# The w_o projection of an encoder block wholly as block products, and two weight sums moved into the FFN

## The chip, the cores and the metric

The kernel runs on one core of one Trainium2 chip. The metric is the device time of one execution in microseconds. A comparison of two kernels is made from several executions of each on the same chip.

## The reference

One trunk layer over 512 frames of 1024 features, in float32:

```python
xn = rmsnorm(h, norm_mix_g)
q, k, v, xr, gr, ga, gb = split(xn @ w_in)
ya = chunked_band_attention(q, k, v, rel_table) @ w_attn_out      # 16 heads of 64
yb = (rg_lru(causal_depthwise_conv(xr, ...)) * gelu(gr)) @ w_rnn_out
h = h + (sigmoid(ga) * ya + sigmoid(gb) * yb) @ w_o               # w_o: 1024 x 1024
g, up = split(rmsnorm(h, norm_ffn_g) @ w_ffn_in)                  # 2 x 2816 columns
h = h + (silu(g) * up) @ w_ffn_out
out = rmsnorm(h, final_norm_g)
```

The change concerns the line with w_o, the norm behind it, and where in time some sums of blocks of w_o and w_ffn_out are made.

## The kernel before

All of it is one program on one core. Products of float32 matrices are made of three passes: an operand is split into a rounded part (hi, by ScalarE, L82) and the rest (lo, by VectorE, L83), and `mm3` (L76 to L78) issues hi x hi, hi x lo, lo x hi on the tensor engine (PE). So every weight block goes through a load by SyncE's queue (SP) into a raw buffer, a split on ScalarE (ACT), a split on VectorE (DVE), and then PE. The raw buffers of the pool wp number three and are used in turn: a load is issued once the split (or the last sum) that read the block three loads earlier is done. Split blocks, called whl, have four buffers in wp, and during the w_o product four more in the pool wop.

Several products are made as block products: a pair of 256-row slices (a "unit") is cut in 2 x 2 blocks, and seven products of blocks or of sums of blocks stand for eight. The sums over the activations (s1 to s4) are made on the spot; the sums over the weights (t1 to t4) are made far ahead by `spill`: four blocks are loaded, four subtractions of 128x1024 run on DVE, and the four results are stored to DRAM, from where `wo_part` or `fo_part` loads them later. Before the change five such spills are made: for the units 0 and 1 of w_ffn_out in the recurrent stage, for w_o and unit 2 of w_ffn_out beside the rnn output product (yb), and for unit 3 beside the attention output product (ya).

The w_o product has 512 tokens (four tiles of 128) and 1024 columns (two halves). Its first 512 rows are a unit, by block products (`h_multiply`); its last 512 rows (two slices, i = 2 and 3) are plain (`plain_h`, `whl_wo`). A bank po_h per token tile and half gathers the sums and `h_read` or `finish_h` adds it to h. Where a token tile has both halves, ACT squares it (hj), DVE adds the two sums (hsq), ACT takes the root (sd), DVE the reciprocal (rs) and scales the tile's rows (xs_ffn, in `scaled`). `turned` then transposes xs_ffn two feature tiles at a time into a bank pt_ffn (two such banks take turns), and ACT and DVE evict it as hn (hi and lo) and x (the whole value). The first FFN products (po_f, weights fg0 and fu0) follow, and the block products of the FFN behind them (p_fg, q_fg, p_fu, q_fu), each with its sums s_fg, s_fu of weight blocks on DVE.

On PE the order is written by hand in the blocks under `manual_schedule`. The order on ACT, DVE and SP is a scheduler's, from the order of the code and its own estimates; each engine runs its rows strictly in that order.

## Time and profile before

| | us |
|---|---|
| median of 3 runs (863.87 to 864.8) | 864.19 |
| the profiled execution's own time | 864.16 |
| its span, first to last instruction | 862.4 |
| PE busy | 850.9 |
| DVE busy | 620.8 |
| ACT busy | 501.7 |

The span and all busy times come from one profiled execution. Lines L.. are those of the kernel; many share the helpers' lines L76 to L83, so groups are told apart by the names of their tiles. A matmul's length in the profile is longer than the distance to the next one, since matmuls overlap.

### The profile page before, as it was taken

The numbers are of one execution on the slowest core, as the hardware profiler recorded it, in microseconds if no ns is written. First come the engines' busy times: TensorE is split into PE (matmuls) and PEld (weight loads), VectorE is DVE, ScalarE is ACT, GpSimd is POOL, SyncE is SP. The second block draws the span as 40 slices with busy tenths as digits, with TensorE's granted clock in tenths as the row PEclk, the third lists the DMA queues.
The fourth block names the chain that finished last, engine by engine and source line by source line (L and its number), as shares of the span: only waits on it lengthen the run. The fifth ranks groups of instructions, "written<-read, shape, count | busy, mean of one in ns | idle before, by whom it ended". The sixth has DMA issues, their size and how long they took to land.

```text
span 862.4 us, 12989 instructions
## 1 busy us (share of the span) xinstructions
PE 850.9 (99%) x4908; PEld 745.6 (86%) x4908; DVE 620.8 (72%) x960; ACT 501.7 (58%) x862; POOL 98.2 (11%) x135
## 2 busy tenths in 40 slices
PE   8999999999999999999999999999999999999996
PEld 6977887888888888888888889999999999988885
DVE  5789866645666666556568968898878887389973
ACT  7577697741366656666634455656556556274543
POOL 2013203200113313223200000000000001000011
PEclk9999999999999999999999999999999999999999
DMA  8585323329842213233187621434333333295602
GB/s 270 183 309 171 98 74 107 113 88 358 271 139 74 73 41 120 74 90 96 49 300 254 202 74 47 126 97 124 104 115 100 99 98 101 82 315 170 195 18 97
DMA packets 93870, 118.91 MB, mean 138 GB/s; under 512 B 6256, under 2 KB 71392, under 8 KB 93808
## 3 DMA queue, kind: packets, MB, share of 16 engines
q1 hardware_dynamic: 90128, 110.42, 39.5%
q10 hardware_dynamic: 3680, 7.67, 2.9%
q8 instruction: 38, 0.62, 0.3%
q14 instruction: 24, 0.20, 0.1%
HBM read 105.45 MB, written 12.62 MB: 137 GB/s over the span
## 4 chain that ended last, share of the span: by engine, by line
PE 95%; ACT 1%; DVE 1%; issue 1%; DMA 1%; SPq 0%; DVEq 0%; ACTq 0%
PE po_out L76 4%; PE po_out L77 4%; PE po_out L78 4%; PE o L745 2%; PE p_fg L78 2%; PE p_fg L77 2%; PE p_fg L76 2%; PE p_fu L78 2%; PE p_fu L77 2%; PE p_fu L76 2%; PE pT L725 2%; PE po_ga L76 2%; PE po_v L76 2%; PE po_ga L78 2%; PE po_q L76 2%; PE po_ya L76 2%
## 5 line engine op out<-in xcount | busy, mean ns | idle before, releaser
L714 POOL TENSOR_SCALAR p<-p,rl 128x128 f32<-128x128 f32 (+1 forms) x64 | 39.6, 638 | 166.4 <-DVE rl L712 166.3
L711 ACT ACTIVATE p<-p,m 128x128 f32<-128x128 f32 (+1 forms) x64 | 35.8, 562 | 14.5 <-DVE m L710 14.5
L1057 POOL TENSOR_TENSOR act_lo<-act,act_hi 128x1024 fp32r<-128x1024 f32 x1 | 2.4, 2405 | 297.2 <-DVE s_fu L175 297.2
L83 DVE TENSOR_TENSOR pp<-pT,pp 128x384 fp32r<-128x384 f32 (+1 forms) x48 | 27.8, 596 | 9.8 <-ACT pp L82 9.7
L710 DVE CUSTOM_DVE_ANT_0 p<-s,bias 128x128 f32<-128x128 f32 (+1 forms) x64 | 29.2, 483 | 3.9 <-PE s L707 3.8
L83 DVE TENSOR_TENSOR whl_qk<-raw_qk,whl_qk 128x1024 fp32r<-128x1024 f32 x16 | 21.5, 1346 | 11.3 <-ACT whl_qk L82 11.3
L82 ACT ACTIVATE whl_fg_s<-s_fg 128x1024 fp32r<-128x1024 f32 x20 | 20.9, 1055 | 14.5 <-PE q_fg L78 5.3
L76 PE MATMUL po_gr<-xnT,whl_gr 128*128 128x512 f32 (+1 forms) x80 | 28.1, 352 | 0.1
L83 DVE TENSOR_TENSOR whl_fu_s<-s_fu,whl_fu_s 128x1024 fp32r<-128x1024 f32 x20 | 24.2, 1224 | 5.3 <-ACT whl_fu_s L82 5.3
L77 PE MATMUL po_xr<-xnT,whl_xr 128*128 128x512 f32 (+1 forms) x80 | 27.8, 353 | 0.0
L77 PE MATMUL po_gr<-xnT,whl_gr 128*128 128x512 f32 (+1 forms) x80 | 27.7, 348 | 0.0
L78 PE MATMUL po_gr<-xnT,whl_gr 128*128 128x512 f32 (+1 forms) x80 | 27.5, 348 | 0.0
L78 PE MATMUL po_xr<-xnT,whl_xr 128*128 128x512 f32 (+1 forms) x80 | 27.3, 346 | 0.0
L76 PE MATMUL po_xr<-xnT,whl_xr 128*128 128x512 f32 (+1 forms) x80 | 26.7, 352 | 0.6 <-ACT xnT L353 0.6
L83 DVE TENSOR_TENSOR whl_fg_s<-s_fg,whl_fg_s 128x1024 fp32r<-128x1024 f32 x20 | 24.2, 1223 | 3.6 <-ACT whl_fg_s L82 3.6
L82 ACT ACTIVATE whl_qk<-raw_qk 128x1024 fp32r<-128x1024 f32 x16 | 16.8, 1051 | 15.6 <-DMA spill<-in_w_ffn_out_dram 7.1
L76 PE MATMUL po_gb<-xnT,whl_gb 128*128 128x512 f32 x64 | 25.1, 393 | 0.5 <-DVE sp_p L452 0.3
L76 PE MATMUL po_ga<-xnT,whl_ga 128*128 128x512 f32 x64 | 25.3, 395 | 0.0
L77 PE MATMUL po_gb<-xnT,whl_gb 128*128 128x512 f32 x64 | 25.2, 394 | 0.0
L83 DVE TENSOR_TENSOR whl_t<-raw_t,whl_t 128x1024 fp32r<-128x1024 f32 x20 | 24.4, 1220 | 1.1 <-ACT whl_t L82 1.0
L78 PE MATMUL po_gb<-xnT,whl_gb 128*128 128x512 f32 x64 | 25.0, 391 | 0.0
L76 PE MATMUL po_q<-xnT,whl_qk 128*128 128x512 f32 x64 | 25.0, 391 | 0.0
(401 smaller groups left out, 3234.4 us busy)
## 6 DMA issues: line engine op xcount, KB each, us to landing
raw_fg<-in_w_ffn_in_dram SPq DMA_DIRECT2D x24, 512.0 KB, 3.5
raw_fu<-in_w_ffn_in_dram SPq DMA_DIRECT2D x22, 512.0 KB, 3.6
spill<-in_w_ffn_out_dram SPq DMA_DIRECT2D x16, 512.0 KB, 6.3
sums<-spill SPq DMA_DIRECT2D x16, 512.0 KB, 3.6
raw_qk<-in_w_in_dram SPq DMA_DIRECT2D x32, 256.0 KB, 3.3
raw_t<-sums SPq DMA_DIRECT2D x16, 512.0 KB, 4.5
raw_b<-in_w_ffn_out_dram SPq DMA_DIRECT2D x12, 512.0 KB, 4.4
raw_xr<-in_w_in_dram SPq DMA_DIRECT2D x8, 512.0 KB, 4.4
```

What stands on the lines that cost most here:

```text
L76: pe.matmul(o, sh, mh, start=start, stop=False, skip_group_check=parts)
L77: pe.matmul(o, sh, ml, start=False, stop=False, skip_group_check=parts)
L78: pe.matmul(o, sl, mh, start=False, stop=stop, skip_group_check=parts)
L82: act.activation(hi, src, AF.Copy)
L83: dve.tensor_sub(lo, src, f(hi))
L710: dve.tensor_tensor_reduce(prob[qb][:], scs[qb], bias[:, S - w:S], -1.0, 3e38, ALU.add, ALU.min, nmax[:, qb:qb + 1])
L711: act.activation(prob[qb][:], prob[qb][:], AF.Exp, bias=nmax[:, qb:qb + 1], scale=-1.0, accum_out=lsum[:, qb:qb + 1])
L714: pool.tensor_scalar(prob[qb][:], prob[qb][:], rl[:, qb:qb + 1], 1.0, ALU.mult, ALU.mult)
L725: pe.transpose(pt[:, at * P:(at + 1) * P], prob[qb][:, kb * P:(kb + 1) * P], ident[:])
L745: pe.matmul(po[:, S - n:S], st, pp[i][:, part, lo:lo + n], start=kb == 0 and part == 0, stop=kb == NT - 1 and part == 1)
L1057: (pool if i == 0 else dve).tensor_sub(lo[:], o[:], f(hi[:]))
```

## The change

The last 512 rows of w_o become a second unit: all of the product is made of block products over two units, and what was plain (`plain_h`) is gone. There are 14 blocks of w_o to load and split (seven for each unit) instead of 11 (seven and four). The products are put in an order in which token tiles 0 and 1 are complete after s4 x b22, with s3 x t3 and a22 x t4 (tiles 2 and 3) behind them; the transposes of the norm stand between the matmuls of these two. There are six spills instead of five: both units of w_o in the recurrent stage, units 0 and 1 of w_ffn_out beside yb, none beside ya, and units 2 and 3 inside the FFN loop, where a generator gives out one subtraction at a time and the tiles come from the pool of the activations.

```diff
@@ -577,7 +577,8 @@
         return [dr.tile([P, 2, S], F32, name=f"{name}_{n}") for n in range(4)]
 
     sums_d = [drams(f"sums{u}") for u in range(len(units))]
-    sums_o = drams("sums_o")
+    units_o = (0, 1), (2, 3)
+    sums_o = [drams(f"sums_o{u}") for u in range(2)]
...
@@ -591,26 +592,29 @@
         for n in range(4):
             sp.dma_start(out=r[n], in_=square(w, unit[n // 2], n % 2))
         b11, b12, b21, b22 = r
-        dve.tensor_sub(b11, b12, b11)
-        dve.tensor_sub(b12, b22, b12)
-        dve.tensor_sub(b22, b22, b11)
-        dve.tensor_sub(b21, b21, b22)
-        for n, i in enumerate((0, 3, 1, 2)):
-            sp.dma_start(out=to[n][:], in_=r[i])
-
-    def spill_of(u, pl, tag, bufs):
-        r = [pl.tile([P, 2, S], F32, tag=tag, bufs=bufs, name=f"spill{u}_{n}")[:] for n in range(4)]
-        if u == "o":
-            spill(w_o, (0, 1), sums_o, r)
-        else:
-            spill(w_ffn_out, units[u], sums_d[u], r)
+        for out_, i, a_, b_ in ((b11, 0, b12, b11), (b12, 2, b22, b12), (b22, 1, b22, b11), (b21, 3, b21, b22)):
+            yield
+            dve.tensor_sub(out_, a_, b_)
+            if out_ is not b11:
+                sp.dma_start(out=to[i][:], in_=out_)
+            if out_ is b22:
+                sp.dma_start(out=to[0][:], in_=b11)
+
+    def spill_of(w, u, pl, tag, bufs):
+        name, unit, to = (("o", units_o, sums_o) if w is w_o else ("f", units, sums_d))
+        r = [pl.tile([P, 2, S], F32, tag=tag, bufs=bufs, name=f"spill{name}{u}_{n}")[:] for n in range(4)]
+        return spill(w, unit[u], to[u], r)
+
+    def at_once(steps):
+        for _ in steps:
+            pass
 
     early_stack, early = opened("early", 4)
 
     conv = {}
     for j in range(0, KT, 2):
         if j >= 4:
-            spill_of(j // 2 - 2, early, "spill", 4)
+            at_once(spill_of(w_o, j // 2 - 2, early, "spill", 4))
         for c in range(2):
             conv[j + c] = rnn_conv(j + c, tile_of(f"xr{j}", c, ahead=2))
         for c in range(2):
@@ -778,7 +782,7 @@
         if j == 6:
             prob = scores(0)
         if j in (0, 3):
-            spill_of(("o", 2)[j // 3], aw, "v", 8)
+            at_once(spill_of(w_ffn_out, j // 3, aw, "v", 8))
         po = mm_tile(f"po_yb{j}")
         project(po, weights(f"yb{j - j % 2}"), j % 2, rnn)
         dve.scalar_tensor_tensor(zB[j], zB[j], 1.0, po[:], ALU.add, ALU.mult)
@@ -802,61 +806,63 @@
 
         raw = wp.tile([P, 2, S], F32, tag="raw", bufs=3, name=f"raw_{name}")
         sp.dma_start(out=raw[:], in_=src)
-        pl = wop if len(wo) < 4 or len(wo) > 7 else wp
+        pl = wp if 4 <= len(wo) < 8 else wop
         hl = pl.tile([P, 2, 2, S], F32R, tag="whl", bufs=4, name=f"whl_{name}")
         split_pair(hl, raw[:])
         wo[name] = hl
 
-    blocks_wo = [("b11", square(w_o, 0, 0)), ("b21", square(w_o, 1, 0)), ("t1", sums_o[0][:]), ("t2", sums_o[1][:]),
-                 ("b22", square(w_o, 1, 1)), ("t3", sums_o[2][:]), ("t4", sums_o[3][:])]
-    blocks_wo += [(f"wo{i}_{cc}", square(w_o, i, cc)) for cc in range(2) for i in (2, 3)]
+    sources = {"b11": (0, 0), "b21": (1, 0), "b22": (1, 1), "t1": 0, "t2": 1, "t3": 2, "t4": 3}
+
+    def blocks_wo(name):
+        n = sources[name]
+        for u in range(2):
+            wo_part(f"{name}_{u}", sums_o[u][n][:] if name[0] == "t" else square(w_o, units_o[u][n[0]], n[1]))
...
-    def m_split(name, src, home):
-        o = home
-        split(o[:, :, 0], o[:, :, 1], src)
-        m_parts[name] = o
-
-    m_parts = {"a11": m_at(0, lo_half), "a12": m_at(1, lo_half), "a22": m_at(1, hi_half)}
+        return za_tiles[2 * u + tile_][:, :, (lo_half, hi_half)[half]]
+
+    def m_sum(name, u):
+
+        op, out, a, b = {"s1": (dve.tensor_add, "22", "21", "22"), "s2": (dve.tensor_sub, "22", "22", "11"),
+                         "s4": (dve.tensor_sub, "12", "12", "22"), "s3": (dve.tensor_sub, "21", "11", "21")}[name]
+        op(m32(out, u), m32(a, u), m32(b, u))
+
+    homes_m = {"a11": (0, lo_half), "a12": (1, lo_half), "a22": (1, hi_half), "s1": (0, hi_half), "s2": (0, lo_half),
+               "s4": (1, lo_half), "s3": (0, hi_half)}
+    m_parts = {(name, u): m_at(2 * u + i, at) for name, (i, at) in homes_m.items() for u in range(2)}
+
+    def m_split(name, u):
+        o = m_parts[name, u]
+        split(o[:, :, 0], o[:, :, 1], m32({"s1": "22", "s2": "22", "s4": "12", "s3": "21"}[name], u))
...
     for j in range(KT):
-        if j >= 4:
-            wo_part(*blocks_wo[j - 4])
-        if j == 5:
-            spill_of(3, aw, "v", 8)
+        if j >= 4 and j % 2 == 0:
+            blocks_wo(("b11", "b21")[j // 2 - 2])
         py = mm_tile(f"po_ya{j}")
         project(py, weights(f"ya{j - j % 2}"), j % 2, aT)
         dve.scalar_tensor_tensor(ta[j], ta[j], 1.0, py[:], ALU.add, ALU.mult)
         dve.tensor_add(ta[j], ta[j], zB[j])
-        at = lo_half if j < 2 else slice(0, S)
+        at = lo_half if j % 4 < 2 else slice(0, S)
         split(mT[j][:, 0, at], mT[j][:, 1, at], ta[j][:, at])
-        if j == 3:
-            m_sum("s1")
-            m_split("s1", m32("22"), m_at(0, hi_half))
+        if j % 4 == 3:
+            m_sum("s1", j // 4)
+            m_split("s1", j // 4)
             for name in ("s2", "s4", "s3"):
-                m_sum(name)
+                m_sum(name, j // 4)
...
-    for name, src in blocks_wo[4:7]:
-        wo_part(name, src)
-    h_tags = {(t, cc): (ss, "s", 2) if cc == 0 and t > 1 else (ps, "t", 2) if cc == 0 else (ps, "mm", 4)
-              for t in range(NT) for cc in range(2)}
+    for name in ("t1", "t2", "b22"):
+        blocks_wo(name)
+    h_tags = {(2, 0): (ss, "s", 2), (3, 0): (ss, "s", 2), (0, 0): (ps, "t", 2), (1, 0): (ps, "t", 2),
+              (0, 1): (ps, "mm", 4), (1, 1): (ps, "mm", 4)}
...
@@ -865,42 +871,60 @@
             bank[t, cc] = pl.tile([P, S], F32, tag=tag, bufs=bufs, name=f"po_h{t}_{cc}")
         return bank[t, cc]
 
-    def h_multiply(a, b, half, cc, start):
-        x, w = m_parts[a], wo[b]
-        for i in range(2):
-            tok = slice(i * P, (i + 1) * P)
-            for k in range(2):
-                mm3(bank_of(2 * half + i, cc)[:], x[:, k, 0, tok], x[:, k, 1, tok], w[:, 0, k], w[:, 1, k],
-                    start and k == 0, k == 1, parts=True)
-
-    def h_read(half, cc, into):
-        for i in range(2):
+    def h_multiply(a, b, half, cc, start, tokens=range(2), us=range(2)):
+        for u in us:
+            x, w = m_parts[a, u], wo[f"{b}_{u}"]
+            for i in tokens:
+                tok = slice(i * P, (i + 1) * P)
+                for k in range(2):
+                    mm3(bank_of(2 * half + i, cc)[:], x[:, k, 0, tok], x[:, k, 1, tok], w[:, 0, k], w[:, 1, k],
+                        start and u == 0 and k == 0, u == 1 and k == 1, parts=True)
...
     with tc.manual_schedule(engines={mybir.EngineType.PE}):
         h_multiply("a11", "b11", 1, 0, True)
-        m_split("s2", m32("22"), m_at(0, lo_half))
+        for u in range(2):
+            m_split("s2", u)
         h_read(1, 0, (0, 0))
         h_multiply("a12", "b21", 0, 0, True)
-        m_split("s4", m32("12"), m_at(1, lo_half))
+        for t in range(2):
+            finish_h(t, 0, False)
+        for u in range(2):
+            m_split("s4", u)
+        blocks_wo("t3")
         h_multiply("s1", "t1", 0, 1, True)
-        m_split("s3", m32("21"), m_at(0, hi_half))
+        for u in range(2):
+            m_split("s3", u)
         h_read(0, 1, (1, 1))
         h_multiply("s2", "t2", 1, 0, False)
         h_read(1, 0, (0, 1))
-        h_multiply("s4", "b22", 0, 1, False)
-        h_multiply("s3", "t3", 1, 0, False)
-        h_read(1, 0, (1, 1))
-        h_multiply("a22", "t4", 1, 0, False)
+        blocks_wo("t4")
...
-    for name, src in blocks_wo[7:]:
-        wo_part(name, src)
     barrier[0] = "fg2"
@@ -954,27 +956,25 @@
     with tc.manual_schedule(engines={mybir.EngineType.PE}):
         xs = []
         for t in range(2):
-            for cc in range(2):
-                for i in (2, 3):
-                    plain_h(t, cc, i)
-                finish_h(t, cc)
+            h_multiply("s4", "b22", 0, 1, False, (t,))
+            finish_h(t, 1, True)
             xs.append(scaled(x32p, ht, hsq, "ffn", t)[0])
         weights("fg0")
-        for cc, i in ((0, 2), (0, 3), (1, 2)):
-            plain_h(2, cc, i)
-        finish_h(2, 0)
+        h_multiply("s3", "t3", 1, 0, False, us=(0,))
+        h_multiply("s3", "t3", 1, 0, False, (0,), us=(1,))
         for jp in (0, 2):
             turned(xs, jp, gf, hn_at, 0, "ffn", f_at)
-        plain_h(2, 1, 3)
-        finish_h(2, 1)
-        for jp, i in ((4, 2), (6, 3)):
-            plain_h(3, 0, i)
+        h_multiply("s3", "t3", 1, 0, False, (1,), us=(1,))
+        h_read(1, 0, (1, 1))
+        for t in (2, 3):
+            square_h(t, 1, False)
+        for u, jp in ((0, 4), (1, 6)):
+            h_multiply("a22", "t4", 1, 0, False, (0,), us=(u,))
             turned(xs, jp, gf, hn_at, 0, "ffn", f_at)
-        finish_h(3, 0)
+        finish_h(2, 0, True)
         xs = [scaled(x32p, ht, hsq, "ffn", 2)[0]]
-        for i in (2, 3):
-            plain_h(3, 1, i)
-        finish_h(3, 1)
+        h_multiply("a22", "t4", 1, 0, False, (1,))
+        finish_h(3, 0, True)
...
@@ -1077,15 +1077,22 @@
     def fo_plain(i, cc):
         plain[i, cc] = fo_part(f"fo{i}_{cc}", fo_block(i, cc))
 
+    def late():
+        for u in (2, 3):
+            yield from spill_of(w_ffn_out, u, acp, "act", 13)
+
+    steps = late()
     for j in range(2, FT, 2):
         if j == FT - 2:
             split_act(0)
             for cc in range(2):
                 fo_plain(0, cc)
+        next(steps, None)
         g, u = (sc.tile([P, 4, 256], F32, tag=f"c{w}", name=f"c_{w}{j}") for w in "gu")
         block_product(f"fg{j}", 0, hn_right, g)
         o = act_tile(j)[:].rearrange("p a b -> p (a b)")
         act.activation(o, g[:].rearrange("p a b -> p (a b)"), AF.Silu)
+        next(steps, None)
         block_product(f"fu{j}", 1, hn_right, u)
         dve.tensor_mul(o, o, u[:].rearrange("p a b -> p (a b)"))
     sc_stack.close()
```

The next rows are DVE's, from the last weights before the norm to the scaling of token tile 1 (h_4388 and h_4389 are tiles 0 and 1 before, h_4382 to h_4384 tiles 0 to 2 now; whl_t is a split of a block of t4, s_fg the sums for the FFN's block product fg2). Before:

```order
L83 TENSOR_TENSOR whl_fg_4_4659<-raw_fg_4_4657,whl_fg_4_4659 128x1024
L937 SCALAR_TENSOR_TENSOR h_4388<-po_h_1_4447,h_4388 128x512
L942 TENSOR_REDUCE hsq_4605<-hsq_0_4586 128x1
L336 RECIPROCAL rs_ffn_4609<-sd_ffn_4607 128x1
L342 TENSOR_SCALAR xs_ffn_4611<-h_4388,rs_ffn_4609 128x1024
L937 SCALAR_TENSOR_TENSOR h_4389<-po_h_0_4438,h_4389 128x512
L83 TENSOR_TENSOR whl_fu_0_4664<-raw_fu_0_4662,whl_fu_0_4664 128x1024
L937 SCALAR_TENSOR_TENSOR h_4389<-po_h_1_4454,h_4389 128x512
L942 TENSOR_REDUCE hsq_4644<-hsq_1_4625 128x1
L336 RECIPROCAL rs_ffn_4648<-sd_ffn_4646 128x1
L342 TENSOR_SCALAR xs_ffn_4650<-h_4389,rs_ffn_4648 128x1024
```

Now:

```order
L897 TENSOR_REDUCE hsq_4622<-hsq_0_4481 128x1
L83 TENSOR_TENSOR whl_t_0_4562<-raw_t_0_4560,whl_t_0_4562 128x1024
L886 SCALAR_TENSOR_TENSOR h_4383<-po_h_1_4509,h_4383 128x512
L336 RECIPROCAL rs_ffn_4626<-sd_ffn_4624 128x1
L83 TENSOR_TENSOR whl_t_1_4567<-raw_t_1_4565,whl_t_1_4567 128x1024
L342 TENSOR_SCALAR xs_ffn_4628<-h_4382,rs_ffn_4626 128x1024
L897 TENSOR_REDUCE hsq_4645<-hsq_1_4485 128x1
L173 TENSOR_TENSOR s_fg_4596<-raw_fg_0_4592,raw_fg_4_4594 128x512
L886 SCALAR_TENSOR_TENSOR h_4384<-po_h_0_4422,h_4384 128x512
L336 RECIPROCAL rs_ffn_4649<-sd_ffn_4647 128x1
L174 TENSOR_TENSOR s_fg_4596<-s_fg_4596,raw_fg_0_4592 128x512
L342 TENSOR_SCALAR xs_ffn_4651<-h_4383,rs_ffn_4649 128x1024
```

The splits of t4, which end the w_o product now, stand between the reads of tile 0 and tile 1 and ahead of both scalings; the sums of fg2, which came before the norm, stand ahead of tile 1's scaling; the splits of fg0 and fu0, which stood here, come later.

ACT's rows in the same place, from tile 1's square (hj) to the evictions of the first transposes. Before:

```order
L939 ACTIVATE hj_1_4642,hsq_1_4625<-h_4389 128x512
L334 ACTIVATE sd_ffn_4646<-hsq_4644,eps_t 128x1
L939 ACTIVATE hj_0_4693,hsq_2_4691<-h_4390 128x512
L353 ACTIVATE hn_4550<-pt_ffn_0_4695,vc 128x256
L353 ACTIVATE hn_4550<-pt_ffn_2_4706,vc 128x256
L356 ACTIVATE x_0_4554<-pt_ffn_0_4695,vc 128x256
L353 ACTIVATE hn_4550<-pt_ffn_0_4695,vc 128x256
L356 ACTIVATE x_1_4555<-pt_ffn_2_4706,vc 128x256
L353 ACTIVATE hn_4550<-pt_ffn_2_4706,vc 128x256
L939 ACTIVATE hj_1_4724,hsq_2_4691<-h_4390 128x512
L82 ACTIVATE whl_fu_4_4669<-raw_fu_4_4667 128x1024
```

Now:

```order
L894 ACTIVATE hj_1_4643,hsq_1_4485<-h_4383 128x512
L334 ACTIVATE sd_ffn_4647<-hsq_4645,eps_t 128x1
L894 ACTIVATE hj_1_4722,hsq_2_4721<-h_4384 128x512
L82 ACTIVATE whl_fg_0_4655<-raw_fg_0_4653 128x1024
L82 ACTIVATE whl_fg_s_4602<-s_fg_4596 128x2x512
L353 ACTIVATE hn_4583<-pt_ffn_0_4691,vc 128x256
L353 ACTIVATE hn_4583<-pt_ffn_2_4702,vc 128x256
L82 ACTIVATE whl_fg_4_4660<-raw_fg_4_4658 128x1024
L356 ACTIVATE x_0_4587<-pt_ffn_0_4691,vc 128x256
L353 ACTIVATE hn_4583<-pt_ffn_0_4691,vc 128x256
L82 ACTIVATE whl_fu_0_4665<-raw_fu_0_4663 128x1024
L356 ACTIVATE x_1_4588<-pt_ffn_2_4702,vc 128x256
```

The first splits of fg0, fg2 and fu0, done before this place until now, stand ahead of and among the evictions of pt_ffn_0 and pt_ffn_2.

DVE's rows in the FFN, where the weights of fg4 are split and summed. Before:

```order
L83 TENSOR_TENSOR whl_fg_a_4985<-raw_fg_4_4980,whl_fg_a_4985 128x512
L83 TENSOR_TENSOR whl_fg_a_4991<-raw_fg_4_4980,whl_fg_a_4991 128x512
L175 TENSOR_TENSOR s_fg_5225<-raw_fg_0_5220 128x512
L173 TENSOR_TENSOR s_fg_5224<-raw_fg_0_5220,raw_fg_4_5222 128x512
L83 TENSOR_TENSOR whl_fg_a_5230<-raw_fg_0_5220,whl_fg_a_5230 128x512
L174 TENSOR_TENSOR s_fg_5224<-s_fg_5224,raw_fg_0_5220 128x512
L83 TENSOR_TENSOR whl_fg_a_5230<-raw_fg_4_5222,whl_fg_a_5230 128x512
L83 TENSOR_TENSOR whl_fg_a_5241<-raw_fg_4_5222,whl_fg_a_5241 128x512
```

Now:

```order
L83 TENSOR_TENSOR whl_fg_a_4984<-raw_fg_4_4979,whl_fg_a_4984 128x512
L83 TENSOR_TENSOR whl_fg_a_4990<-raw_fg_4_4979,whl_fg_a_4990 128x512
L597 TENSOR_TENSOR spillf_0_5096<-spillf_1_5097,spillf_0_5096 128x1024
L175 TENSOR_TENSOR s_fg_5233<-raw_fg_0_5228 128x512
L597 TENSOR_TENSOR spillf_1_5097<-spillf_3_5099,spillf_1_5097 128x1024
L597 TENSOR_TENSOR spillf_3_5099<-spillf_3_5099,spillf_0_5096 128x1024
L83 TENSOR_TENSOR whl_fg_a_5238<-raw_fg_0_5228,whl_fg_a_5238 128x512
L289 TENSOR_TENSOR c_g_5104<-keepb_fg_5133 128x256
L597 TENSOR_TENSOR spillf_2_5098<-spillf_2_5098,spillf_3_5099 128x1024
L173 TENSOR_TENSOR s_fg_5232<-raw_fg_0_5228,raw_fg_4_5230 128x512
L290 TENSOR_TENSOR c_g_5104<-q_fg_5131,keepa_fg_5132 128x512
L83 TENSOR_TENSOR whl_fg_a_5238<-raw_fg_4_5230,whl_fg_a_5238 128x512
```

The four subtractions of unit 2 (spillf) stand among the splits and sums of fg4. Unit 3's follow in the same manner 39 rows later.

43 lines of the change are left out of this document (16 added, 27 removed).

## The prediction

> **What bounds the kernel now.** I read the page first, then the table of busy time by stretch, then single rows of the timeline in the stretch that the change rebuilds. The page says that the tensor engine sets the time:
>
> ```profile
> PE 850.9 (99%) x4908; PEld 745.6 (86%) x4908; DVE 620.8 (72%) x960; ACT 501.7 (58%) x862; POOL 98.2 (11%) x135
> PE 95%; ACT 1%; DVE 1%; issue 1%; DMA 1%; SPq 0%; DVEq 0%; ACTq 0%
> ```
>
> PE is busy for 99% of the span and makes 95% of the chain that ended last. So there is nearly no wait left to gain: a matmul taken out gives its time back, and each new wait of PE is a loss. By stretch (start:end, then busy us and instructions of PE, weight loads, DVE, ACT, POOL, then clock, DMA share, GB/s):
>
> ```profile
> 432.00:476.00 44.00, 44.00 (x198) 36.50 (x197) 34.84 (x44) 18.01 (x23) 0.00 (x0) 1.00 0.80 274
> 476.00:500.00 24.00, 24.00 (x107) 19.90 (x106) 21.38 (x29) 11.42 (x16) 0.00 (x0) 1.00 0.64 201
> 500.00:519.00 19.00, 18.72 (x91) 15.34 (x90) 12.48 (x25) 11.90 (x28) 0.00 (x0) 1.00 0.25 78
> 533.00:560.00 27.00, 27.00 (x228) 27.00 (x227) 23.07 (x34) 16.26 (x27) 0.00 (x0) 1.00 0.38 118
> 560.00:600.00 40.00, 40.00 (x336) 40.00 (x335) 35.93 (x50) 24.36 (x44) 0.00 (x0) 1.00 0.34 106
> 600.00:700.00 100.00, 100.00 (x835) 100.00 (x835) 82.18 (x115) 55.82 (x103) 0.00 (x0) 1.00 0.34 106
> ```
>
> The w_o product and the second norm lie from 476 to 519; PE idles there 0.28 us in all, at full clock. DVE has slack, but in the FFN only 4.07 us of 40 from 560 to 600.
>
> **The change, part by part.**
>
> *Twelve matmuls fewer.* The second half of w_o's rows took 4 token tiles x 2 halves x 2 pairs x 2 x 3 = 96 matmuls; as seven products it takes 84. The timeline shows what one is worth (start, length):
>
> ```profile
> 475.99 0.39 PE L76 MATMUL po_h<-whl_b,mT 128*128 128x512 f32 x1
> 500.02 0.39 PE L76 MATMUL po_h<-whl_t,mT 128*128 128x512 f32 x1
> 502.51 0.39 PE L78 MATMUL po_h<-whl_t,mT 128*128 128x512 f32 x1
> 519.12 0.28 PE L76 MATMUL po_f<-hn,whl_fg 128*128 128x256 f32 x1
> ```
>
> The first and last of twelve in a row start 2.49 us apart, 0.2265 us each; the 0.39 us is a length, and lengths overlap. So 12 x 0.2265 = **-2.7 us**; 12 x 0.39 = 4.7 would count the overlap as time.
>
> The Trainium skill (TensorE: Matmul & The Clock Gate, Back-to-back issue gap) gives about 131 ns per 512-column matmul in a sustained stream; by that the twelve would give back only 1.6 us. This trace disagrees, at 0.2265, and I go by the trace.
>
> *The last products before the norm.* I count from the first matmul of the w_o product (h+0, 475.99 above). Before, the last read ahead of the transposes went so:
>
> ```profile
> 499.65 1.28 ACT L334 ACT_TABLE_LOAD   x1
> 500.95 0.30 ACT L334 ACTIVATE sd_ffn<-hsq,eps_t 128x1 f32<-128x1 f32 x1
> 505.91 0.39 PE L76 MATMUL po_h<-whl_wo,mT 128*128 128x512 f32 x1
> 506.11 0.69 DVE L937 SCALAR_TENSOR_TENSOR h<-po_h,h 128x512 f32<-128x512 f32 x1 [0.81 <-PE po_h L78]
> 506.90 0.63 ACT L939 ACTIVATE hj<-h 128x512 f32<-128x512 f32 x1 [2.00 <-DVE h L937]
> 507.65 0.15 DVE L942 TENSOR_REDUCE hsq<-hsq 128x1 f32<-128x2 f32 x1 [0.85 <-ACT hj L939]
> 507.84 0.29 ACT L334 ACTIVATE sd_ffn<-hsq,eps_t 128x1 f32<-128x1 f32 x1 [0.22 <-DVE hsq L942]
> 508.17 0.16 DVE L336 RECIPROCAL rs_ffn<-sd_ffn 128x1 f32<-128x1 f32 x1 [0.36 <-ACT sd_ffn L334]
> 508.37 0.75 DVE L342 TENSOR_SCALAR xs_ffn<-h,rs_ffn 128x1024 f32<-128x1024 f32 x1
> 510.00 0.27 PE L349 MATMUL pt_ffn<-ident,xs_ffn 128*128 128x128 f32 x1
> 514.08 0.63 PE L349 MATMUL pt_ffn<-ident,xs_ffn 128*128 128x128 f32 x4 [0.28 <-ACT hj L939]
> ```
>
> Token tile 1 was complete at 505.9, its scaled rows at 509.1: 3.2 us, hidden behind 18 matmuls (4.1 us), with 0.9 us to spare. The new code keeps 18 matmuls of cover (six matmuls per unit and tile of s3 x t3), but not the empty engines. In the new order t4's two block splits, the table load and the sums for fg2 stand between tile 1's read and its scaling. Their prices, with transfers from the page's part 6:
>
> ```profile
> L83 DVE TENSOR_TENSOR whl_t<-raw_t,whl_t 128x1024 fp32r<-128x1024 f32 x4 | 4.9, 1222 | 0.3 <-ACT whl_t L82 0.3
> L82 ACT ACTIVATE whl_t<-raw_t 128x1024 fp32r<-128x1024 f32 x4 | 4.2, 1060 | 1.0 <-DMA raw_t<-sums_o 1.0
> L173 DVE TENSOR_TENSOR s_fg<-raw_fg,raw_fg 128x512 f32<-128x512 f32 x1 | 0.7, 694 | 0.0
> L354 DVE SCALAR_TENSOR_TENSOR hn<-pt_ffn,vc,hn 128x256 fp32r<-128x256 f32 x16 | 7.5, 479 | 3.4 <-ACT hn L353 3.4
> L353 ACT ACTIVATE hn<-pt_ffn,vc 128x256 fp32r<-128x256 f32 x16 | 7.4, 472 | 3.3 <-PE pt_ffn L349 3.2
> raw_fg<-in_w_ffn_in_dram SPq DMA_DIRECT2D x24, 512.0 KB, 3.5
> raw_wo<-in_w_o_dram SPq DMA_DIRECT2D x4, 512.0 KB, 3.4
> raw_fo<-in_w_ffn_out_dram SPq DMA_DIRECT2D x6, 512.0 KB, 4.6
> ```
>
> Back-to-back rows start some 0.09 before the one ahead ends. Walked along the new order:
>
> 1. Tile 0 is complete after 96 + 12 = 108 matmuls, h+24.5; DVE reads it 0.2 later, ACT has squared it at 26.1.
> 2. ACT next splits t4's first block, whose room b22's first block leaves at matmul 114 (25.8): 26.15 to 27.2. Then the table load to 28.4, the root to 28.7, t4's second block to 29.75, and only then tile 1's square, to 30.4.
> 3. DVE follows ACT: t4's first block 27.2 to 28.45. Tile 1, complete at 27.2, is read behind it, 28.4 to 29.05. Second block 29.8 to 31.0, tile 0's scaling to 31.65, tile 1's sum 31.75; its root on ACT at 32.05.
> 4. Ahead of tile 1's reciprocal stands a sum over raw_fg, whose second half goes into the buffer that t4's first block leaves at 28.45; plus 3.5 it lands at 32.0. Sum to 32.7, a read of tile 2 to 33.3, reciprocal, another sum to 34.0, scaling to 34.7.
>
> PE wants these transposes after 138 matmuls, h+31.3. It waits 0.4 for tile 0, transposes, and waits 2.8 for tile 1: **+3.2 us**.
>
> *The third group of transposes* needs a bank that the first has left; only two take turns. But fg0's weights, loaded into buffers freed at 31.0 and 34.05, land at 34.5 and 37.55, and their splits stand among the evictions. ACT: fg0's first half to 35.6, fg2's sums to 36.6, evictions to 37.4, fg0's second half to 38.6, evictions to 39.4. DVE: 36.9, 38.0, 38.8, 39.95, a read to 40.55, the bank's last two evictions to 41.35. PE, after 0.6 us of transposes and 12 matmuls behind 34.7, is there at 38.0: 3.3 us, less the 0.28 that it waited before: **+3.1 us**.
>
> *The rest of the norm.* Tiles 2 and 3 are scaled behind a sum that waits for raw_fu in turn; their transposes come late, and the fourth group a little: by the same walk **+0.5 us** (0 if the loads land early, 1.5 if each takes 1 us more).
>
> *The earlier products.* Three more blocks are split, and s1 to s4 made for a second unit, DVE and ACT work under PE. Walked likewise, the nearest is s2 of unit 1: split at h+14.25, wanted at 19.0. Zero, with 4.8 us of cover. That w_ffn_out's fourth sums leave 432 to 476 saves DVE four rows and the queues 4 MB where PE waits for nothing: zero.
>
> *Two units' sums inside the FFN.* Eight 128x1024 subtractions (1.14 us apart, 9.1 in all) and sixteen 512 KB transfers. From 533 to 700 DVE has 25.8 us free, but unit 2's four come where 40 us have 4.07 free: 4.6 against 4.07, about **+0.3 us**, for late weights. Between 0 (all hidden) and 4.6 (all four on PE's path). SP's queue holds weight loads behind the stores, which wait for the subtractions; those loads wait for DVE's buffers anyway.
>
> **Sum.** -2.7 + 3.2 + 3.1 + 0.5 + 0.3 = +4.4. The profiled execution took 864.16 us for a span of 862.4, the median is 864.19: **868.5 us**. Transfers landing a microsecond sooner save 1.3 of the waits (867.2); at 4.4 instead of 3.5 (raw_fo above has 4.6) the two loads that follow each other on the path cost 1.8 and the FFN 0.8 more (871.1).
>
> **Rivals.**
>
> - *Only the matmuls count.* The splits and loads finish under the cover, PE loses no new time: 864.16 - 2.7 - 0.3 = 861.2. It decides if what stands between tile 1's read and its scaling costs under 0.9 us more than before. For it: ACT and DVE are far from full (11.90 and 12.48 of 19 us). Against: the rows in that order alone are two splits and a table load.
> - *One wait instead of two.* Weights for fg0 land before the evictions are due, so that only the first wait is left: 864.16 - 2.7 + 3.2 + 0.3 = 865.0, no change. It needs raw_fg's load well under the row's 3.5 us.
> - *The FFN becomes DVE's.* All four of unit 2's subtractions fall on PE's path, on top of the sum: 868.5 + 4.3 = 872.8. For it: 90% DVE from 560 to 600. Against: 18 us free behind.
> - *A dearer table switch.* If the engine stood still as long again around the load, tile 1's root would come 1.3 us later: 869.8. The rows show none of it, 1.30 from the load's start to the root's.
>
> The Trainium skill (ScalarE: Activation LUTs, What ACT_TABLE_LOAD costs) adds about 1380 ns of drain to each load of 1283 ns; this trace shows the 1.28 and no drain, so that rival gets little.
>
> **How the numbers follow.** Forecast 0.72, matmuls only 0.06, one wait 0.09, FFN 0.10, table 0.03. A measurement of this kernel tells about 0.2% (1.7 us) from no change. Faster 0.06; same 0.10 (one wait, and a sliver of the forecast); slower 0.84. The range runs from 865.2, which takes in the early loads and part of the one-wait case, to 871.4, past the late loads; the FFN rival's upper part and the fast one lie outside.
>
> **What would show it.** In the changed kernel's profile PE should have idle time of some 3 us ahead of the first pt_ffn, released by DVE xs_ffn, and some 3 us ahead of the third group, released by DVE's x; the distance from the first po_h matmul to the first po_f should grow from 43.1 to about 46.8 us in spite of twelve matmuls fewer. From there to the first po_out it should grow by under 1 us. A PE without waits at pt_ffn would make the forecast wrong, and so would waits at p_fg or p_fu that add up to more than 1.5 us.

## The result, and the profile after

The changed kernel takes **869.38 us** in the median of four runs (868.6 to 871.49), against 864.18 before: a ratio of 1.0063, with a 95% interval of 1.0044 to 1.0082. It is slower by 5.2 us, though it has twelve matmuls fewer. The forecast was 868.5 in a range of 865.2 to 871.4.

The profiled execution is the slowest of the four: 871.49 us for a span of 869.7. Its page, part 1 and the chain that ended last:

```profile
PE 851.7 (98%) x4896; PEld 746.2 (86%) x4896; DVE 632.4 (73%) x973; ACT 505.5 (58%) x869; POOL 97.8 (11%) x135
PE 93%; DMA 2%; DVE 2%; ACT 2%; issue 1%; DVEq 0%; ACTq 0%
```

The tensor engine is busy a little *longer* with twelve instructions fewer, and its share of the chain fell from 95% to 93%. Where it waited (engine, line, releaser: us in all, times, longest):

```profile
PE pt_ffn L349 <- DVE xs_ffn L342: 2.6, 1, 2.6
PE po_f L77 <- DVE hn L354: 2.0, 1, 2.0
PE pt_ffn L349 <- ACT whl_fu L82: 1.6, 1, 1.6
```

Three marks cut the time into stages: the first matmuls of po_h, po_f and p_fg, and the last of po_out. The timeline of the change has them at

```profile
476.07 0.39 PE L76 MATMUL po_h<-whl_b,mT 128*128 128x512 f32 x1
522.88 0.28 PE L76 MATMUL po_f<-hn,whl_fg 128*128 128x256 f32 x1
551.44 0.28 PE L76 MATMUL p_fg<-hn,whl_fg_a 128*128 128x256 f32 x1
861.88 0.28 PE L78 MATMUL po_out<-whl_t,x_a 128*128 128x256 f32 x1
```

and that of the kernel before, whose first two marks the forecast shows (475.99 and 519.12), at

```profile
544.14 0.28 PE L76 MATMUL p_fg<-hn,whl_fg_a 128*128 128x256 f32 x1
854.59 0.28 PE L78 MATMUL po_out<-whl_t,x_a 128*128 128x256 f32 x1
```

| from | to | before | after | difference | forecast |
|---|---|---|---|---|---|
| first po_h | first po_f | 43.13 | 46.81 | +3.68 | +3.6 |
| first po_f | first p_fg | 25.02 | 28.56 | +3.54 | +0.5 |
| first p_fg | last po_out | 310.45 | 310.44 | 0 | +0.3 |

So the w_o product and the norm lost what was forecast, the first FFN products lost 3 us more, and the long FFN lost nothing. Stretches of the change (busy us and instructions of PE, weight loads, DVE, ACT, POOL, then granted clock, DMA share, GB/s) show a thing that no term of the forecast has. The granted clock is the tensor engine's, as a share of its full speed:

```profile
510.70:514.20 3.50, 3.44 (x12) 3.01 (x13) 3.13 (x5) 3.19 (x5) 0.00 (x0) 0.52 0.73 207
514.20:517.40 3.20, 1.72 (x8) 1.09 (x6) 3.14 (x6) 2.20 (x5) 0.00 (x0) 1.00 0.91 275
525.60:527.70 2.10, 0.07 (x1) 0.00 (x0) 1.14 (x3) 0.00 (x0) 0.00 (x0) 1.00 0.02 5
527.70:531.10 3.40, 3.40 (x16) 3.40 (x17) 2.55 (x7) 1.78 (x3) 0.00 (x0) 0.50 0.00 0
531.10:532.10 1.00, 1.00 (x11) 1.00 (x10) 0.00 (x0) 0.48 (x2) 0.00 (x0) 0.99 0.00 0
551.40:861.60 310.20, 310.20 (x2165) 291.66 (x2164) 253.20 (x339) 172.13 (x290) 7.50 (x5) 1.00 0.46 153
```

Behind each of the two long waits the tensor engine runs at half its clock for some 3.4 us (the second time 0.50 up to 531.10 and 0.99 after it), with other engines and transfers in quite different states (DMA share 0.73 and 0.00).

### The profile page after: what moved, and what is told of

The parts are those of the page before. It is cut to its first block, busy times and chain, and to the rows that moved or that the text cites. A ratio compares the mean times of both kernels' runs of the same rounds, so it can differ in the third digit from the quotient of the medians.

```text
span 869.7 us, 13005 instructions
## 1 busy us (share of the span) xinstructions
PE 851.7 (98%) x4896; PEld 746.2 (86%) x4896; DVE 632.4 (73%) x973; ACT 505.5 (58%) x869; POOL 97.8 (11%) x135
## 4 chain that ended last, share of the span: by engine, by line
PE 93%; DMA 2%; DVE 2%; ACT 2%; issue 1%; DVEq 0%; ACTq 0%
PE po_out L78 4%; PE po_out L77 4%; PE po_out L76 4%; PE o L749 2%; PE p_fu L77 2%; PE p_fg L77 2%; PE p_fu L78 2%; PE p_fg L78 2%; PE p_fg L76 2%; PE p_fu L76 2%; PE pT L729 2%; PE po_ga L76 2%; PE po_v L76 2%; PE po_q L76 2%; PE po_ga L78 2%; PE po_k L76 2%
## 5 line engine op out<-in xcount | busy, mean ns | idle before, releaser
L83 DVE TENSOR_TENSOR whl_t<-raw_t,whl_t 128x1024 fp32r<-128x1024 f32 x24 | 29.3, 1219 | 4.1 <-ACT whl_t L82 4.1
L82 ACT ACTIVATE whl_t<-raw_t 128x1024 fp32r<-128x1024 f32 x24 | 25.1, 1049 | 6.8 <-PE po_out L78 4.0
L597 DVE TENSOR_TENSOR spillf<-spillf,spillf 128x1024 f32<-128x1024 f32 x16 | 19.5, 1221 | 11.7 <-DMA spillf<-in_w_ffn_out_dram 11.7
L83 DVE TENSOR_TENSOR whl_b<-raw_b,whl_b 128x1024 fp32r<-128x1024 f32 x18 | 21.9, 1218 | 6.6 <-ACT whl_b L82 6.4
L82 ACT ACTIVATE whl_b<-raw_b 128x1024 fp32r<-128x1024 f32 x18 | 18.9, 1051 | 12.1 <-DMA raw_b<-in_w_o_dram 11.5
L76 PE MATMUL po_gb<-xnT,whl_gb 128*128 128x512 f32 x64 | 25.1, 393 | 0.5 <-DVE sp_p L452 0.3
```

Of the source, the lines that this page charges most:

```text
L76: pe.matmul(o, sh, mh, start=start, stop=False, skip_group_check=parts)
L82: act.activation(hi, src, AF.Copy)
L83: dve.tensor_sub(lo, src, f(hi))
L597: dve.tensor_sub(out_, a_, b_)
```

## The experiments

**The change once more**, unaltered, in five runs.

> The changed kernel itself, unaltered, to see what of its time is the same in every execution. In the profiled execution of the change the tensor engine's clock fell to 0.52 for the 3.5 us behind the 2.6 us wait at the first transposes, and to 0.57 for the 4 us behind a 2.0 us wait inside po_f; both waits follow from the order. Theory A (the waits bring the slow clock): every execution has the waits, a clock of 0.994 to 0.996 over the span where both stretches are slow and 0.998 where none is, and a time of about 868.6 with none, 870 to 871.5 with both; median 869 to 870. Theory B (that execution was disturbed by something else): the clock is 0.998 in most executions and the times lie within 0.5 us of 868.6.

Measured: 868.98 us (868.67 to 870.21), ratio 1.0061 (1.0049 to 1.0074). The trace of one of them (span 867.2, mean clock 0.995) has these waits, and in its po_f stretch (first row) and its FFN (second):

```profile
PE pt_ffn L349 <- DVE xs_ffn L342: 2.9, 2, 2.5
PE pt_ffn L349 <- DVE x L358: 1.5, 1, 1.5
PE po_f L77 <- DVE hn L354: 0.5, 1, 0.5
```

```profile
522.70:548.90 26.20, 25.33 (x209) 24.77 (x208) 22.29 (x41) 16.55 (x32) 0.00 (x0) 1.00 0.12 36
548.90:859.10 310.20, 310.20 (x2165) 291.64 (x2164) 253.15 (x339) 172.15 (x290) 7.47 (x5) 1.00 0.46 153
```

The waits of the norm are the same within 0.1 us. The wait inside po_f is 0.5 instead of 2.0, no slow stretch follows it, and the stretch from po_f to p_fg grows by 1.2 us instead of 3.5. Neither theory fits whole. All five have a mean clock of 0.994 to 0.996, where the kernel before has 0.997 to 0.999 in 51 of 52 runs beside these experiments, which speaks for a slow stretch in all of them (of the first four runs one had 0.998, and that was the shortest, 868.6). Between the two traces the wait inside po_f differs, and with it the slow clock behind it. How much of the spread in time that makes is not shown: the longest of the five, 870.21, has the highest mean clock, 0.996.

**The idle places filled** with matmuls into a bank that nothing reads.

```diff
+            if name == "fg0" and c == 0 and half == 0 and k == KT - 1:
+                fill(8)
...
+    def fill(n):
+        for _ in range(n):
+            pe.matmul(dummy[:], m_parts["s3", 0][:, 0, 0, 0:P], wo["t3_0"][:, 0, 0], start=True, stop=True)
...
+        fill(12)
         for jp in (0, 2):
             turned(xs, jp, gf, hn_at, 0, "ffn", f_at)
...
+            fill(12 if u == 0 else 0)
```

> The change with extra matmuls into a bank that nothing reads, put where the tensor engine stands idle: 12 ahead of the first pt_ffn, 12 ahead of the third group, 8 ahead of the po_f matmul that waited 2.0 us (0.2265 us each). They add no result. Theory A (idling lowers the clock): the granted clock stays at 1.00 all through the norm. Behind the first wait nothing is gained, since the third group waits for a bank that comes free at 41.4 us after the first po_h either way; behind the second wait 22 matmuls and 8 transposes go at 0.12 instead of 0.21, so the distance from the first to the last po_f falls from 28.4 to about 27, and the time by 1 to 1.5 us, to some 868.3. Theory B (the slow stretches come from something else there, such as the transfers under way): the clock still falls in the same places, and the extra matmuls cost 0 to 1 us: 869.4 to 870.5.

Measured: 869.62 us (869.29 to 869.76), mean clock 0.997 or 0.998 in all five. The norm and the po_f stretch:

```profile
507.00:523.00 16.00, 15.26 (x76) 12.10 (x75) 14.94 (x27) 11.61 (x24) 0.00 (x0) 1.00 0.70 219
523.00:549.00 26.00, 26.00 (x213) 25.66 (x212) 21.99 (x40) 16.35 (x31) 0.00 (x0) 1.00 0.10 31
```

With the engine kept busy the clock stays at 1.00 while transfers and the other engines do what they did: it was the idling. Theory A is right about the clock and wrong about the time, which did not fall to 868.3. The traces give two reasons. The third group starts 41.3 us after the first po_h here, 41.4 in the change; so the slow matmuls of the norm had only used up time in which the engine would have waited for a bank. And eight matmuls (1.8 us) gain where the wait inside po_f is 2.0 us, not where it is 0.5: from po_f to p_fg it takes 26.6 us here, against 28.6 and 26.2 in the two traces of the change.

**The sums for fu2 later**, and with it **t4's blocks in a room of their own**: the second kernel has both edits.

```diff
+            if name == "fu2":
+                with tc.issue_after(mark[0]):
+                    dve.tensor_add(s1, a21, a22)
...
-        dve.tensor_scalar(xsc[:], src[t][:], rs[:, 0:1], None, ALU.mult)
+        mark[0] = dve.tensor_scalar(xsc[:], src[t][:], rs[:, 0:1], None, ALU.mult).ins
```

```diff
+        if name[:2] == "t4":
+            pl, tag, bufs = ((x32p, "hn01", 1), (hnp, "hn11", 1))[int(name[3])]
...
-        blocks_wo("t4")
...
+    blocks_wo("t4")
```

> The change, with one order changed on the vector engine: the first of fu2's sums (s_fu over raw_fu) may only follow the scaling of tile 3 instead of standing ahead of the evictions, of xs_ffn of tiles 2 and 3. My account: the 2.0 us wait of po_f for hn was that sum, waiting for its load, in front of hn on the same engine. Then this wait goes, with the slow clock behind it (1.5 us); the first waits at pt_ffn stay at 2.6 to 2.8 and the third group's end at 41.1 to 41.4 us after the first po_h. Time 866 to 868.2. Rival (the vector engine is simply full there, so that a wait goes and another takes its place): po_f still waits 1.5 us or more in all, time 869 to 870.

> As the run with fu2's sums later, and t4's two blocks are split into the room of hn's second halves, which is empty until then, instead of into buffers that b22's blocks leave. So t4 needs not wait for the s4 x b22 products and its splits stand ahead of the read of tile 0, not between tile 1's read and its scaling. My account (the two waits come from what stands in the order between that read and the scaling, and from fg0's splits among the evictions): the first wait shrinks to some 2.3 us (fg0's splits move up and take part of the place), the third group's to nothing; the distance from the first po_h to the first po_f falls from 46.8 to about 42.3 us and the time to 863.6, 864.5 where the clock falls behind the first wait. Rival (moving t4 only moves the queue, the vector engine's work in the norm being the bound): the distance stays at 45 us or more and the time above 866.

Measured: 867.46 us (867.2 to 867.66; ratio 1.0039, 1.0025 to 1.0053) with fu2's sums later, and 865.03 (863.76 to 866.47, eleven runs; ratio 1.0011, 1.0002 to 1.002) with t4 moved too. The waits of the first at the norm and a stretch behind the longer one, then the same of the second, which has no other wait there:

```profile
PE pt_ffn L354 <- DVE xs_ffn L347: 2.4, 1, 2.4
PE pt_ffn L354 <- DVE x L363: 0.5, 1, 0.5
510.00:516.80 6.80, 6.11 (x18) 4.97 (x18) 6.14 (x9) 5.53 (x10) 0.00 (x0) 0.50 0.75 230
```

```profile
PE pt_ffn L354 <- DVE xs_ffn L347: 2.5, 2, 2.3
510.00:513.60 3.60, 3.48 (x13) 2.88 (x14) 3.02 (x7) 3.07 (x9) 0.00 (x0) 0.64 0.73 212
```

In the first, po_f no longer waits, and the times lie within 0.5 us though the mean clocks go from 0.994 to 0.997. The sum waiting for its load in front of hn was the cause, worth 1.5 us against the change in the same set of runs. The third group waits 0.5 instead of 1.5, but starts at 41.6 us all the same: the slow clock lasted 6.8 us here instead of 3.4, and more of the time ahead of the group went by at it. In this trace the slow clock thus takes the place of a wait, and adds little to the time; the other four were not profiled.

In the second, the first wait shrinks to 2.3 and the third group's is gone, both as expected, but the distance from the first po_h to the first po_f is 44.5 instead of 42.3: now no wait follows that hides the slow clock. The time lies 0.5 us above the 864.5 that was expected at the most, and 1 below the rival's 866. Without a wait it would be 40.1 (43.1 before, less its 0.3 us wait and 2.7 for the matmuls); waits of 2.5 us in all cost 4.4. The executions of this kernel sort by their clock: 863.8 to 864.8 at 0.997 to 0.999 (three), 865.0 to 866.5 at 0.994 to 0.996 (eight).

**Twelve matmuls fewer**, alone, in the kernel before.

```diff
+        ks = 1 if b in ("b11", "b21") else 2
...
-            for k in range(2):
+            for k in range(ks):
...
```

> The kernel before the change, with twelve matmuls left out and nothing else: in the first two products of w_o only the first of two pairs of rows is multiplied (so half of these two products is missing from the result). This is the price of the first term by itself. By the row (0.2265 us from start to start) the time falls by 2.7 us to 861.4; by the length of a matmul (0.39) it would fall by 4.7 to 859.5; at 131 ns, the figure of the Trainium skill (TensorE: Matmul & The Clock Gate, Back-to-back issue gap), by 1.6 to 862.6. Rival: the norm behind it is bound by the vector engine's work or the loads already, so that nothing or less than 1.5 us comes back: above 862.7.

Measured: 861.53 us against 864.25, ratio 0.9969 (0.9957 to 0.9981): -2.7 us. The distance between starts is the price (what the kernel leaves out is half of two products), and the norm before the change had room for all of it. By the Trainium skill (TensorE: Matmul & The Clock Gate, Back-to-back issue gap), with its 131 ns for such a matmul in a sustained stream, the estimate would be 1.6 us: too little for these.

**t4's splits and fg2's sums behind the scaling**, with the orders of the vector and scalar engines held to the text.

> The change, with tensor, vector and scalar engine held to the written order around the first two scalings: read, square, root and scaling of tiles 0 and 1 first, then t4's two splits, the sums for fg2 and fg0's splits. So nothing stands between tile 1's read and its scaling. My account, walked along the new order: the first wait is gone (transposes at 31.3 us after the first po_h), but the same work now stands ahead of the first group's evictions; the third group still waits 3 us, po_f0 waits 2.5 us for its weights and hn, tiles 2 and 3 come 1 us late. Sum +0.9 against the change, and 1 to 2 more where the clock falls: 870 to 871.5. Rival (the place in the order is all that was wrong): the first wait's 3 us are gained, 866.

Measured: 870.09 us (869.73 to 872.83), ratio 1.0075 (1.0062 to 1.0088). In its timeline the first transposes start without a wait, and the third group takes the wait over, with a slow clock behind it (the last row is a stretch):

```profile
506.93 1.34 PE L349 MATMUL pt_ffn<-ident,xs_ffn 128*128 128x128 f32 x8
513.93 1.09 PE L349 MATMUL pt_ffn<-ident,xs_ffn 128*128 128x128 f32 x4 [2.90 <-DVE x L358]
513.20:520.00 6.80, 6.07 (x19) 5.03 (x20) 6.69 (x12) 3.90 (x6) 0.00 (x0) 0.50 0.54 178
```

The rival falls: it is not only the place in the order. In that stretch the vector engine is busy for 6.69 of 6.80 us (in the change for 8.72 of 8.90, from 514.0 to the first po_f), so whatever is put behind the scaling stands ahead of the evictions. What helps is work that leaves the stretch, as t4's splits did above.

**The order mended further**: fu0's splits behind the second group's evictions; and the same with the two units' sums out of the FFN.

```diff
+            if jp == 2:
+                with tc.issue_after(emark[0]):
+                    weights("fu0", 0)
```

```diff
         if j >= 4:
             at_once(spill_of(w_o, j // 2 - 2, early, "spill", 4))
+        else:
+            at_once(spill_of(w_ffn_out, 2 + j // 2, early, "spill", 4))
...
     def late():
-        for u in (2, 3):
-            yield from spill_of(w_ffn_out, u, acp, "act", 13)
+        yield
```

> As the run with t4 in its own room (and fu2's sums late), with one thing more: fu0's two splits may only follow the evictions of the second group of transposes, and so no longer stand ahead of tile 1's scaling. Walked along the order: the tensor engine waits 0.4 and 1.2 us at the first transposes and 0.6 at the third group; no wait is over 1.5 us. Theory A (only a wait of about 2 us or more brings the slow clock): no slow stretch, first po_h to first po_f 41.8 us, time 863.1 (1.1 below before). Theory B (any idling brings it): 1 to 1.6 us more, 864.2 to 864.8.

> As the run with the order mended, and the fourth term undone: the two units' sums of w_ffn_out are made in the first projections, beside those of w_o, instead of inside the FFN. My forecast charged the FFN 0.3 us for them; the traces of the change show 310.2 us from the first p_fg to the last po_out, against 310.3 before, that is nothing. Theory A (they cost 0 to 0.3): the time is that of the run with the order mended, or up to 0.4 less, 862.7 to 863.1. Theory B (the FFN was the vector engine's, only hidden by the late start): 1 to 4 us less. Theory C (the sums hurt where they are put): the projections at the start get longer, the first po_h later than 476.3.

Measured: 863.34 us (862.97 to 864.94; ratio 0.9992, 0.9984 to 1.0001) for the first, 869.65 (868.69 to 870.73; ratio 1.0065, 1.0052 to 1.0077) for the second. The waits of the first at the norm, and what is new in the second:

```profile
PE pt_ffn L355 <- DVE xs_ffn L348: 1.5, 2, 1.0
PE pt_ffn L355 <- DVE x L364: 0.3, 1, 0.3
```

```profile
PE rg L519 <- POOL xch L501: 3.8, 2, 3.2
483.39 0.39 PE L76 MATMUL po_h<-whl_b,mT 128*128 128x512 f32 x1
```

The first has 42.3 us from the first po_h to the first po_f, 43.1 before: of the 2.7 us that the matmuls save, waits of 1.8 (before 0.3) took most. Its profiled execution has a mean clock of 0.999, as theory A has it, and the median lies 0.2 above A's 863.1; but two of the eleven executions have 0.995, 864.35 and 864.94 us, and their waits are not known. The median is 0.9 us below the kernel before, with an interval that just includes no change, so it is not shown to be faster. In the second the FFN is as long as ever (310.4 us from the first p_fg to the last po_out in both), and the first projections are 7.6 us longer (first po_h at 483.4 instead of 475.8): the sums cost nothing inside the FFN and much where they compete with the projections. So the sums' price in the FFN is nothing, as theory A has it, but its time of 862.7 to 863.1 is missed by 7 us because theory C came true; B falls.

**How long an idle tensor engine costs**: three kernels of the before, with tile 1's scaling repeated (the loop is `range(3)`, `range(5)`, `range(8)`).

```diff
+        for _ in range(3 if (name, t) == ("ffn", 1) else 0):
+            dve.tensor_scalar(xsc[:], src[t][:], rs[:, 0:1], None, ALU.mult)
```

> The kernel before the change, with tile 1's scaling done four times instead of once (the same values written again, 0.67 us each), so that the tensor engine idles ahead of the first transposes. By the walk it stands still for 1.6 us, at a point where it had run at full clock for the whole w_o product, and the end comes 1.4 later. Theory A (a wait under some 2 us leaves the clock alone): granted clock 0.997 to 0.998, time 865.6. Theory B (any wait brings the slow clock): clock 0.996, 867.2.

> As the run with tile 1's scaling done four times, but six times: a wait of 3.2 us by the walk, the end 3.8 later by it. Theory A (a wait of over 2 us brings some 3.5 us at half clock, worth 1.6 to 1.8 us, unless another wait swallows it): the matmuls behind the first transposes start 0.43 us apart instead of 0.2265, clock 0.996 or less, time 868 (without any later wait) to 869.7. Theory B (the clock has nothing to do with the wait): 868.0 with a clock of 0.998.

> As the run with tile 1's scaling done four times, but nine times: a wait of 5.5 us by the walk, the end 6.1 later by it. Theory A: the slow stretch behind the wait is as long as behind a shorter one (3.4 to 4 us), so the price over the wait itself stays at 1.6 to 1.8 us: 870.3 to 872.1. Theory C (the slow stretch grows with the wait): 3 us or more over the wait, 873 or above. Theory B: 870.3 with a clock of 0.998.

Measured: 865.95, 869.33 and 871.50 us, against 864.12. The first transposes behind the wait and two matmuls soon after, of the short, the middle and the long one:

```profile
512.05 0.87 PE L351 MATMUL pt_ffn<-ident,xs_ffn 128*128 128x128 f32 x6 [1.64 <-DVE xs_ffn L344]
513.23 0.40 PE L78 MATMUL po_h<-whl_wo,mT 128*128 128x512 f32 x1
513.46 0.40 PE L76 MATMUL po_h<-whl_wo,mT 128*128 128x512 f32 x1
```

```profile
513.52 1.54 PE L351 MATMUL pt_ffn<-ident,xs_ffn 128*128 128x128 f32 x6 [3.21 <-DVE xs_ffn L344]
515.72 0.63 PE L78 MATMUL po_h<-whl_wo,mT 128*128 128x512 f32 x1
516.14 0.63 PE L76 MATMUL po_h<-whl_wo,mT 128*128 128x512 f32 x1
```

```profile
515.72 1.54 PE L351 MATMUL pt_ffn<-ident,xs_ffn 128*128 128x128 f32 x6 [5.57 <-DVE xs_ffn L344]
517.91 0.63 PE L78 MATMUL po_h<-whl_wo,mT 128*128 128x512 f32 x1
518.34 0.63 PE L76 MATMUL po_h<-whl_wo,mT 128*128 128x512 f32 x1
```

The slow clock of the middle one, which begins within its wait:

```profile
512.70:519.60 6.90, 6.08 (x18) 5.02 (x19) 4.13 (x9) 3.13 (x8) 0.00 (x0) 0.51 0.01 2
```

After 1.6 us the matmuls keep their 0.23 us distance and the time rises by 1.8; after 3.2 and 5.6 us they start 0.42 to 0.43 apart and it rises by 5.2 and 7.4, 2.0 and 1.8 us more than the wait. The price over the wait does not grow with it (theory C falls). The times are theory A's, but not the length: in these two traces the clock is low for some 6.8 us, of which 6.1 and 5.7 lie behind the wait, instead of the 3.4 to 4 expected. Not every execution pays it: of the four with the middle wait one has a mean clock of 0.998 and takes 868.45 us, near theory B's 868.0.

**Half of fg0's and fu0's splits on GpSimd**, on top of the kernel with t4 in a room of its own. A second edit goes with it: the instruction that is there to bring the root's table in early now reads a tile that is made late (it ran at 2.9 us in the change and runs at 491.9 here).

```diff
+                elif name in ('fg0', 'fu0'):
+                    act.activation(hl[:, 0], raw[:], AF.Copy)
+                    pool.tensor_sub(hl[:, 1], raw[:], f(hl[:, 0]))
...
-    act.activation(warm[:], eps_t[:], AF.Sqrt)
+    act.activation(warm[:], q2s[1][:, 0:1], AF.Sqrt)
```

> As the run with t4 in its own room (and fu2's sums late), and the second half of fg0's and fu0's splits (four subtractions of 128x1024) is done by GpSimd, which stands idle in this stretch, instead of the vector engine; the table load for the root follows the first squares instead of standing between tile 0's square and its root. GpSimd's one such row takes 2.4 us against 1.22 on the vector engine. Theory A (the vector engine's work between the last read and the first transposes is the bound): waits of 0.5 and 1.0 us are left by the walk, first po_h to first po_f 41.2 us, 862.5 to 862.8, 1.4 to 1.7 below before. Theory B (GpSimd's work slows the vector engine, or comes too late for po_f): waits at po_f or longer rows of the vector engine while GpSimd works, 863.3 or more.

Measured: 863.44 us (862.85 to 866.51), ratio 1.0001 (0.9991 to 1.0011): no change from the kernel before is shown. The median is 1.6 us below that of the kernel it was made from (865.03); which of the two edits brought that, no run shows. It misses theory A's 862.8 by 0.6 and lies in B's range: the first wait is 1.3 us where 0.5 was forecast, and from the first po_h to the first po_f it takes 42.7 instead of 41.2. Two rows of GpSimd's work, and beside them the scalings of tiles 0 and 1, which take 0.74 to 0.75 in the other traces:

```profile
502.95 2.40 POOL L247 TENSOR_TENSOR whl_fg<-raw_fg,whl_fg 128x1024 fp32r<-128x1024 f32 x1 [78.41 <-DVE hsq L907]
503.98 1.92 DVE L350 TENSOR_SCALAR xs_ffn<-h,rs_ffn 128x1024 f32<-128x1024 f32 x1
505.52 2.61 POOL L247 TENSOR_TENSOR whl_fg<-raw_fg,whl_fg 128x1024 fp32r<-128x1024 f32 x1 [0.18 <-ACT whl_fg L246]
507.45 1.23 DVE L350 TENSOR_SCALAR xs_ffn<-h,rs_ffn 128x1024 f32<-128x1024 f32 x1
```

The first scaling took 1.92 us and ended 0.55 us behind GpSimd's row. The Trainium skill (SBUF — State Buffer, Who interferes with whom) has GpSimd and such a vector instruction take turns at one pair of ports, the later one standing still until the earlier is done; this row agrees. Tile 1's scaling, which the first transposes wait for, took 1.23 us and also ended 0.55 us behind a GpSimd row. So part of what was taken off the vector engine came back as its own scalings being held.

## Why the forecast was right, and where it was not

**Twelve matmuls, -2.7.** Right: -2.7 in the run with that alone.

**The first wait, +3.2.** Right in place, cause and nearly in size: 0.24 and 2.58 us, and none where t4's splits and fg2's sums stand behind the scaling. The vector engine's rows of the change, walked beside the forecast's step 3 and 4 (476.07 is the zero):

```profile
504.38 0.68 DVE L886 SCALAR_TENSOR_TENSOR h<-po_h,h 128x512 f32<-128x512 f32 x1
505.80 1.23 DVE L83 TENSOR_TENSOR whl_t<-raw_t,whl_t 128x1024 fp32r<-128x1024 f32 x1 [0.67 <-ACT whl_t L82]
508.09 0.69 DVE L173 TENSOR_TENSOR s_fg<-raw_fg,raw_fg 128x512 f32<-128x512 f32 x1 [0.34 <-DMA raw_fg<-in_w_ffn_in_dram]
509.96 0.75 DVE L342 TENSOR_SCALAR xs_ffn<-h,rs_ffn 128x1024 f32<-128x1024 f32 x1
```

Tile 1 is read at 28.3 (forecast 28.4), the sum over raw_fg starts at 32.0 (32.0, when its load lands), tile 1 is scaled at 34.6 (34.7).

**The third group, +3.1.** Its start was right: 517.48 - 476.07 = 41.41 us, forecast 41.35. So was its cause, though the list of waits of the first trace names ACT's split of fu0, which ended last before it: the eviction that the forecast names, and to which the second trace puts the wait, ended 0.15 us ahead of the group in both.

```profile
516.86 0.47 DVE L358 TENSOR_SCALAR x<-pt_ffn,vc 128x256 f32<-128x256 f32 x1
```

But only 1.57 of the 3.1 is idling; most of the rest went to the transposes ahead of it and the first five of the 12 matmuls, which ran at half clock. That the size came out is partly luck: the wait for the bank hid the slow clock, and the run with t4 moved shows what it costs where nothing hides it.

**The rest of the norm, +0.5 (0 to 1.5).** This is the step that was mis-sized: 3.5 us in the profiled execution, 1.2 in the other trace, and the forecast's own sign for it, under 1 us from the first po_f to the first po_out, failed in both. The forecast put the sum over raw_fu ahead of the scaling of tiles 2 and 3 and overlooked what else is queued behind it:

```profile
526.56 0.69 DVE L173 TENSOR_TENSOR s_fu<-raw_fu,raw_fu 128x512 f32<-128x512 f32 x1 [2.79 <-DMA raw_fu<-in_w_ffn_in_dram]
527.17 0.48 DVE L354 SCALAR_TENSOR_TENSOR hn<-pt_ffn,vc,hn 128x256 fp32r<-128x256 f32 x1
```

That hn is the last eviction of the first half, and po_f needs it. The load went out as fu0's second split ended, at about 520.7, and landed at 526.5: 5.8 us, where the forecast took 3.5 and allowed 4.4. In the other trace it took 4.2 and landed at 524.8; why the same load takes 1.6 us longer in one execution no run shows. So the wait is 2.0 or 0.5. What is left over the longer one, 1.5 (3.5 - 2.0), is about what 3.4 us at half clock cost, 1.7.

**The earlier products, 0,** and **the FFN, +0.3.** Both measured as nothing. (The difference that the forecast names for the second, 4.6 against 4.07, is 0.5 and not 0.3.) The first po_h is 0.08 later; from the first p_fg on the distance is the same to 0.01 us, though the vector engine works more there, 253.20 us against

```profile
544.10:854.40 310.30, 310.30 (x2166) 291.71 (x2165) 244.84 (x331) 172.16 (x290) 7.47 (x5) 1.00 0.39 126
```

before: the cover held.

**The rivals.** Only the matmuls, one wait, and the FFN as the vector engine's all fell. So did the dearer table switch: the load starts at 503.22 and the root at 504.52, 1.30 later, as before.

**What was missing** is the granted clock. The forecast priced a wait of the tensor engine at its length and had no rival for what follows it. Here a wait of 2.0 us or more mostly brought a further 1.5 to 2.0 us of slow matmuls, unless a later wait swallowed it. That the median came out 0.9 us above the forecast fits the mis-sized term (+0.7 in the second trace) and what of the clock was not hidden; only two of the nine executions have a trace.
